# Splitting the weights behind the mixers once and keeping both parts in DRAM, in a hybrid decoder layer

## The chip, the cores and the metric

One core of a Trainium2 chip runs the whole program. The metric is device time in microseconds (us) from one launch. Before the change three runs took 3306.91, 3300.41 and 3303.79 us; the median is 3303.79. The profile comes from one more execution of 3299.76 us.

## The reference, cut to what matters

One layer of a decoder trunk over 2048 prompt tokens (and 8 sample tokens, one step each), width 1024:

```python
x = x + concat[mLSTM heads, S5 channel groups, gated-DeltaNet heads](rmsnorm(x) @ w_in) @ w_out
x = x + cross_attn(x)      # 4 heads into 256 memory tokens: softmax(q k) v, then w_mo
x = x + (silu(h @ w_gate) * (h @ w_up)) @ w_down      # h = rmsnorm(x), inner width 2816
y = rmsnorm(x)
```

Everything is float32. The mixers carry a state along the tokens; the S5 output also passes a gate with the weights w_glu. What comes behind the mixers (w_glu, w_out, cross attention, FFN) works on each token alone, with the same weights for all tokens.

## The kernel before, in words

The prompt is cut into four segments of 512 tokens, and the activations lie feature by token, so a weight tile of 128 partitions is the stationary operand of a matmul and up to 512 tokens stream past it. First come the memory keys and values and the w_in products of all four segments (`win`), with two folds in between that multiply memory keys and values into w_mq and w_mo (results Ad and Bd, in DRAM). Then `post` runs four times, once for each segment: w_glu, w_out, scores and values with Ad and Bd, then the FFN in six chunks of four or three tiles of gate and up, each chunk followed by its part of w_down. The mixers (`mlstm`, `gdn`, `s5`) and the attention of the sample tokens are generators; `tick` steps them between the matrix products, so that their small operations fall beside the large ones. In the trace post(0) runs from about 836 us, post(1) from 1483, post(2) from 2162 and post(3) from 2759 to the end. The mixers of segments 1, 2 and 3 and half of S5 run beside post(0), post(1) and post(2); beside post(3) there are none.

A float32 product is made of three float32r products: both operands are split into a high part (rounded to float32r) and a low part (the rest), and `gemm3` computes high x high, high x low and low x high into one PSUM tile. So each weight tile of up to 128 x 1024 is loaded raw into `wr` (L286 to L289), cast into `wh` on ScalarE (L292), and the low part `wl` is the difference wr - wh, on GpSimd or, for the first two tiles and those of index over 360, on VectorE (L293). `wr`, `wh` and `wl` have three buffers each. All weight tiles stand in one list `WL` of 512 entries in the order of use: 116 for `win`, memory and folds, then 103, 103, 95 and 95 for the four posts. `load_w` hands out tile i, makes the split of tile i + 2 and starts raw loads up to two tiles ahead of that. So a weight used in all four posts is loaded and split four times.

All transfers are issued by SyncE (SP), one queue whose instructions go in the order in which they stand; an instruction that waits holds those behind it. The order of each engine's instructions is set when the program is built, by a scheduler with a model of times; loads and splits of weights are put in with raised priority (`HP`). On the chip each engine then keeps its order and waits on semaphores.

Names: `H`, `X` are split activations, `x` the residual tiles, `t` temporaries, `acc` sums of squares, `P` and `M` PSUM tiles, `TB`, `big`, `g`, `m`, `mR` mixers' tiles, `gyd` and `mixd` the mixers' outputs in DRAM. L152 is `TT` (tensor_tensor on any engine), L155 `STT` (scalar_tensor_tensor on VectorE), L164 `mm`.

Of the kernel before, what the change touches and what calls it, by code (L numbers as in the profile page):

```python
# [6 lines left out]
F32 = mybir.dt.float32  # L7
# [6 lines left out]
MUL, ADD, SUB, MAX, MIN, POW = ALU.mult, ALU.add, ALU.subtract, ALU.max, ALU.min, ALU.pow  # L14
# [52 lines left out]
def build(ctx, tc, I, O):  # L67
    nc = tc.nc
    V, S, G, PE, SY = nc.vector, nc.scalar, nc.gpsimd, nc.tensor, nc.sync
# [14 lines left out]
    def nm(s):  # L84
        uid[0] += 1
        return f"{s}{uid[0]}"
# [4 lines left out]
    def dtile(shape, name):  # L91
        return dr.tile(shape, F32, name=name, tag=name)
# [58 lines left out]
    def TT(eng, out, a, b, op):  # L151
        eng.tensor_tensor(out=out, in0=a, in1=b, op=op)  # L152
# [64 lines left out]
    Ad = dtile([8, 128, 1024], "Ad")  # L217
    Bd = dtile([8, 128, 1024], "Bd")
# [49 lines left out]
    WL, wst, raws, splits = [], {"r": 0, "s": 0, "u": 0}, {}, {}  # L268

    def w_raw():  # L270
        with tc.high_priority(offset=HP):
            w_raw_()

    def w_split():
        with tc.high_priority(offset=HP):
            w_split_()

    def w_raw_():
        i = wst["r"]
        src, n = WL[i]  # L280
        raw = wp.tile([128, WN], F32, name=nm("wr"), tag="wr", bufs=3)
        src(raw)
        raws[i] = raw
        wst["r"] += 1

    def w_split_():  # L286
        i = wst["s"]
        n = WL[i][1]
        raw = raws.pop(i)  # L289
        wh = wp.tile([128, WN], F32R, name=nm("wh"), tag="wh", bufs=3)  # L290
        wl = wp.tile([128, WN], F32R, name=nm("wl"), tag="wl", bufs=3)
        S.copy(wh[:, 0:n], raw[:, 0:n])  # L292
        TT(V if i < 2 or i > 360 else G, wl[:, 0:n], raw[:, 0:n], wh[:, 0:n].bitcast(F32), SUB)  # L293
        splits[i] = (wh, wl)
        wst["s"] += 1

    def load_w():
        i = wst["u"]
        wst["u"] += 1
        while wst["s"] <= i + 2 and wst["s"] < len(WL):  # L300
            while wst["r"] <= wst["s"] + 2 and wst["r"] < len(WL):
                w_raw()
            w_split()
        return splits.pop(i)

    def plain(src, n=1024):
        WL.append((lambda raw: SY.dma_start(raw[:, 0:n], src), n))

    def gemm3(P, n, W, wofs, X, b0, bn, ks, mid=None, m=128, first=True, last=True):
        wh, wl = W  # L310
# [70 lines left out]
    def wl_win(extra=None):  # L381
        for n in range(18):
            plain(I["wF"][n])
            if extra is not None:
                extra(n)
        for g0, g1_ in ((0, 3), (3, 6), (6, 8)):
            plain(I["wTM"][:, g0:g1_, :].rearrange("p k c -> p (k c)"), (g1_ - g0) * 272)

    pre = {}
# [1069 lines left out]
    def wl_mem(i):  # L1459
        plain(I["wmk"][i] if i < 8 else I["wmv"][i - 8])  # L1460
# [3 lines left out]
    def mem_load():  # L1464
        mem["x"] = []
        for kk in range(4):
            x = xt()
            SY.dma_start(x[:, 0:512].rearrange("p (k c) -> p k c", k=2),
                         I["memT"][kk * 256:(kk + 1) * 256, :].rearrange("(k p) c -> p k c", p=128))
            mem["x"].append(x)  # L1470
            if kk in (0, 2):
                w_raw_()
# [89 lines left out]


    def wl_post(seg):
        for n in range(2):
            plain(I["wglu"][n])
        for n in range(8):
            plain(I["wout"][n])

        for h in range(4):  # L1570
            for i in range(2):
                plain(Ad[2 * h + i])
            for i in range(2):
                if seg == 0:
                    plain(I["wmq"][h, i])
                if seg == 1:
                    plain(I["wmo"][h, i])
        for n in range(3):
            plain(Bd[n, :, 0:768], 768)
        WL.append((lambda raw: SY.dma_start(raw[:, 0:768].rearrange("p (n c) -> p n c", n=3),  # L1580
                                            Bd[0:3, :, 768:1024].rearrange("n p c -> p n c")), 768))
        for n in range(3, 8):
            plain(Bd[n])
        for ci, (f0, fn) in enumerate(FCH):
            for f in range(f0, f0 + fn):
                if f != f0 or ci == 0:
                    plain(I["wgate"][f])
                plain(I["wup"][f])
            if ci + 1 < len(FCH):
                plain(I["wgate"][f0 + fn])  # L1590
            for n in range(0, 8, 2):
                def dn(raw, n=n, f0=f0, fn=fn):
                    SY.dma_start(raw[:, 0:2 * fn * 128].rearrange("p (a m) -> p a m", a=2),
                                 I["wdown"][n:n + 2, :, f0 * 128:(f0 + fn) * 128].rearrange("a p m -> p a m"))
                WL.append((dn, 2 * fn * 128))

    def hsplit(src, T, scale=None):
        h, l = ht(), ht()
# [368 lines left out]
    for i in range(NSEG):  # L1967
        wl_post(i)
# [265 lines left out]
```

## Time and profile before

| what | value |
|---|---|
| median of three runs | 3303.79 us |
| profiled execution | 3299.76 us, span 3298.0 us |
| PE busy | 3063.1 us, 93% of the span, 18202 matmuls |
| PEld, weight loads into PE | 2619.2 us, 79% |
| DVE busy | 2337.6 us, 71% |
| ACT busy | 1114.5 us, 34% |
| POOL busy | 1103.8 us, 33% |
| mean granted TensorE clock | 0.966 |
| DMA | 451.58 MB, mean 137 GB/s; the hardware queue 45.7% of 16 engines |

A busy share is the part of the span in which an engine had an instruction under way. Matmuls are pipelined, so two of them overlap and a busy PE is not always a PE at its peak. The clock is the granted share of the full TensorE clock, a mean over a stretch between the two levels of 2.4 GHz (1.00) and 1.2 GHz (0.50). The DMA share is the mean over the 16 DMA engines of the time that their packets took.

### The profile page before, as it was taken

The numbers are of one execution on the slowest core, as the hardware profiler recorded it, in microseconds if no ns is written. First come the engines' busy times: TensorE is split into PE (matmuls) and PEld (weight loads), VectorE is DVE, ScalarE is ACT, GpSimd is POOL, SyncE is SP. The second block draws the span as 40 slices with busy tenths as digits, with TensorE's granted clock in tenths as the row PEclk, the third lists the DMA queues.
The fourth block names the chain that finished last, engine by engine and source line by source line (L and its number), as shares of the span: only waits on it lengthen the run. The fifth ranks groups of instructions, "written<-read, shape, count | busy, mean of one in ns | idle before, by whom it ended". The sixth has DMA issues, their size and how long they took to land.

```text
span 3298.0 us, 49267 instructions
## 1 busy us (share of the span) xinstructions
PE 3063.1 (93%) x18202; PEld 2619.2 (79%) x18202; DVE 2337.6 (71%) x4746; ACT 1114.5 (34%) x1882; POOL 1103.8 (33%) x706
## 2 busy tenths in 40 slices
PE   7777889999888998998999999989999999999998
PEld 6676678778877776787789999978777877888886
DVE  8783695786788689668886787687766767554445
ACT  3123433422542332234432322244324224332222
POOL 6332545534354444444544444344411000000000
PEclk9887999999999999999999999999999999999999
DMA  6679666666445345335443444352333325222332
GB/s 208 176 183 206 205 184 212 200 193 173 144 129 182 90 122 166 103 111 168 144 121 117 125 124 125 100 164 84 105 94 108 104 90 182 88 91 95 96 90 77
DMA packets 361361, 451.58 MB, mean 137 GB/s; under 512 B 144820, under 2 KB 246556, under 8 KB 361120
## 3 DMA queue, kind: packets, MB, share of 16 engines
q1 hardware_dynamic: 361120, 448.43, 45.7%
q8 instruction: 144, 2.36, 0.3%
q14 instruction: 97, 0.79, 0.1%
HBM read 378.73 MB, written 71.73 MB: 137 GB/s over the span
## 4 chain that ended last, share of the span: by engine, by line
PE 61%; DVE 13%; issue 3%; ACT 2%; DMA 2%; SPq 0%; POOL 0%; DVEq 0%; POOLq 0%; ACTq 0%
PE P L164 54%; PE M L164 5%; DVE t L155 3%; DVE big L152 3%; DVE x L152 1%; DVE s5h L155 1%; DVE TB L155 1%; DVE acc L152 1%; ACT wh L292 1%; DMA t<-mixd 1%; DVE x L155 1%; DVE H L152 0%; DVE H L155 0%; DMA x<-in_xT 0%; DMA ABd<-AW 0%
## 5 line engine op out<-in xcount | busy, mean ns | idle before, releaser
L164 PE MATMUL P<-H,wh 128*128 128x512 f32 (+2 forms) x8032 | 2190.0, 360 | 80.1 <-DVE t L152 32.7
L164 PEld LDWEIGHTS P<-H,wh 128*128 128x128 f32 x8032 | 1419.4, 191 | 309.4 <-issue 30.9
L164 PE MATMUL P<-H,wl 128*128 128x512 f32 (+2 forms) x4016 | 1430.8, 357 | 13.8 <-POOL wl L152 13.8
L152 POOL TENSOR_TENSOR wl<-wr,wh 128x1024 fp32r<-128x1024 f32 (+2 forms) x359 | 863.5, 2409 | 970.4 <-ACT wh L292 861.7
L292 ACT CAST wh<-wr 128x1024 fp32r<-128x1024 f32 (+3 forms) x512 | 521.1, 1020 | 1198.1 <-PE P L164 705.1
L164 PEld LDWEIGHTS P<-H,wl 128*128 128x128 f32 x4016 | 766.9, 191 | 124.6 <-POOL wl L152 16.3
L152 DVE TENSOR_TENSOR x<-x,P 128x512 f32<-128x512 f32 (+2 forms) x312 | 181.2, 587 | 141.9 <-PE P L164 128.9
L152 DVE TENSOR_TENSOR big<-big,big 32x87 f32<-32x87 f32 (+16 forms) x500 | 249.6, 499 | 18.7 <-DMA big<-ABd 10.8
L164 PE MATMUL P<-wh,H 128*128 128x256 f32 (+1 forms) x1280 | 244.6, 289 | 8.2 <-ACT pp L1717 6.3
L152 DVE TENSOR_TENSOR t<-P,R 128x512 f32<-128x512 f32 (+2 forms) x190 | 109.6, 581 | 165.7 <-PE P L164 142.0
L152 POOL TENSOR_TENSOR rs<-rcol,mhalf 128x4 f32<-128x4 f32 (+2 forms) x17 | 20.7, 1218 | 598.5 <-DVE rcol L161 598.2
L164 PEld LDWEIGHTS P<-wh,H 128*128 128x128 f32 x1280 | 204.7, 193 | 12.0 <-ACT pp L1717 8.2
L152 DVE TENSOR_TENSOR wl<-wr,wh 128x1024 fp32r<-128x1024 f32 (+1 forms) x153 | 183.8, 1202 | 25.5 <-ACT wh L292 22.8
L164 PE MATMUL P<-wl,H 128*128 128x256 f32 (+1 forms) x640 | 183.0, 287 | 0.5 <-POOL wl L152 0.5
L155 DVE SCALAR_TENSOR_TENSOR t<-P,R 128x512 f32<-128x512 f32 (+1 forms) x120 | 69.6, 583 | 153.9 <-PE P L164 152.2
L155 DVE SCALAR_TENSOR_TENSOR t<-t,t 128x512 f32<-128x512 f32 (+3 forms) x140 | 146.7, 1052 | 37.5 <-ACT t L1830 23.2
L152 DVE TENSOR_TENSOR H<-t,H 128x512 fp32r<-128x512 f32 (+1 forms) x120 | 123.5, 1037 | 46.3 <-ACT H L1600 46.2
L164 PEld LDWEIGHTS P<-wl,H 128*128 128x128 f32 x640 | 123.6, 193 | 1.2 <-POOL wl L152 0.7
L1600 ACT CAST H<-t 128x512 fp32r<-128x512 f32 (+1 forms) x120 | 73.5, 621 | 141.7 <-DVE t L152 124.8
L155 DVE SCALAR_TENSOR_TENSOR t<-g,VEC,t 128x256 f32<-128x256 f32 x144 | 99.5, 691 | 20.0 <-ACT t L724 18.4
L155 DVE SCALAR_TENSOR_TENSOR H<-x,VEC,H 128x512 fp32r<-128x512 f32 (+2 forms) x104 | 102.2, 996 | 8.5 <-ACT H L334 6.6
L152 DVE TENSOR_TENSOR acc<-acc,t 128x512 f32<-128x512 f32 (+1 forms) x115 | 99.1, 861 | 9.2 <-ACT t L343 7.3
(414 smaller groups left out, 3114.7 us busy)
## 6 DMA issues: line engine op xcount, KB each, us to landing
wr<-in_wgate SPq DMA_DIRECT2D x88, 512.0 KB
wr<-in_wup SPq DMA_DIRECT2D x88, 512.0 KB
wr<-in_wF SPq DMA_DIRECT2D x72, 512.0 KB
wr<-in_wdown SPq DMA_DIRECT2D x64, 512.0 KB
TB<-TB SPq DMA_DIRECT2D x64, 417.0 KB
wr<-in_wout SPq DMA_DIRECT2D x32, 512.0 KB
wr<-Ad SPq DMA_DIRECT2D x32, 512.0 KB
zf<-t SPq DMA_DIRECT2D x56, 256.0 KB
```

Source lines behind the costliest of these rows:

```text
L152: eng.tensor_tensor(out=out, in0=a, in1=b, op=op)
L155: V.scalar_tensor_tensor(out=out, in0=a, scalar=s, in1=b, op0=op0, op1=op1, **kw)
L164: PE.matmul(out, l, r, start=st, stop=sp)
L292: S.copy(wh[:, 0:n], raw[:, 0:n])
L1600: S.copy(h[:, 0:T], src[:, 0:T])
```

## The change

The weights of the posts that every segment uses (w_glu, w_out, Ad, Bd, w_gate, w_up, w_down: 95 tiles of a post) are split in post(0) only. There both parts are also stored into DRAM tiles `ws_...` (mode "store"). In post(1), post(2) and post(3) no raw tile is loaded for them; both parts are loaded from DRAM, straight into `wh` and `wl` (mode "pre"). The tiles of `win`, memory and folds, and the eight tiles of wmq in post(0) and of wmo in post(1), keep their raw load and their split (mode "raw"). Subtractions that are left go to GpSimd but for the first two tiles.

```diff
--- before.py
+++ after.py
@@ -277,22 +277,38 @@
 
     def w_raw_():
         i = wst["r"]
-        src, n = WL[i]
+        wst["r"] += 1
+        src, n, key, mode = WL[i]
+        if mode == "pre":
+            return
         raw = wp.tile([128, WN], F32, name=nm("wr"), tag="wr", bufs=3)
         src(raw)
         raws[i] = raw
-        wst["r"] += 1
 
     def w_split_():
         i = wst["s"]
-        n = WL[i][1]
-        raw = raws.pop(i)
+        src, n, key, mode = WL[i]
         wh = wp.tile([128, WN], F32R, name=nm("wh"), tag="wh", bufs=3)
         wl = wp.tile([128, WN], F32R, name=nm("wl"), tag="wl", bufs=3)
-        S.copy(wh[:, 0:n], raw[:, 0:n])
-        TT(V if i < 2 or i > 360 else G, wl[:, 0:n], raw[:, 0:n], wh[:, 0:n].bitcast(F32), SUB)
+        if mode == "pre":
+            for q, t in enumerate((wh, wl)):
+                SY.dma_start(t[:, 0:n].bitcast(F32), wsd(key, n)[q])
+        else:
+            raw = raws.pop(i)
+            S.copy(wh[:, 0:n], raw[:, 0:n])
+            TT(V if i < 2 else G, wl[:, 0:n], raw[:, 0:n], wh[:, 0:n].bitcast(F32), SUB)
+            if mode == "store":
+                for q, t in enumerate((wh, wl)):
+                    SY.dma_start(wsd(key, n)[q], t[:, 0:n].bitcast(F32))
         splits[i] = (wh, wl)
         wst["s"] += 1
+
+    WSD = {}
+
+    def wsd(key, n):
+        if key not in WSD:
+            WSD[key] = dtile([2, 128, n], "ws_" + "_".join(str(q) for q in key))
+        return WSD[key]
 
     def load_w():
         i = wst["u"]
@@ -303,8 +319,8 @@
             w_split()
         return splits.pop(i)
 
-    def plain(src, n=1024):
-        WL.append((lambda raw: SY.dma_start(raw[:, 0:n], src), n))
+    def plain(src, n=1024, key=None, mode="raw"):
+        WL.append((lambda raw: SY.dma_start(raw[:, 0:n], src), n, key, mode))
 
     def gemm3(P, n, W, wofs, X, b0, bn, ks, mid=None, m=128, first=True, last=True):
         wh, wl = W
@@ -1562,37 +1578,37 @@
 
 
     def wl_post(seg):
+        mode = "store" if seg == 0 else "pre"
         for n in range(2):
-            plain(I["wglu"][n])
+            plain(I["wglu"][n], key=("u", n), mode=mode)
         for n in range(8):
-            plain(I["wout"][n])
-
+            plain(I["wout"][n], key=("o", n), mode=mode)
         for h in range(4):
             for i in range(2):
-                plain(Ad[2 * h + i])
+                plain(Ad[2 * h + i], key=("A", 2 * h + i), mode=mode)
             for i in range(2):
                 if seg == 0:
                     plain(I["wmq"][h, i])
                 if seg == 1:
                     plain(I["wmo"][h, i])
         for n in range(3):
-            plain(Bd[n, :, 0:768], 768)
+            plain(Bd[n, :, 0:768], 768, ("B", n), mode)
         WL.append((lambda raw: SY.dma_start(raw[:, 0:768].rearrange("p (n c) -> p n c", n=3),
-                                            Bd[0:3, :, 768:1024].rearrange("n p c -> p n c")), 768))
+                                            Bd[0:3, :, 768:1024].rearrange("n p c -> p n c")), 768, ("B", 8), mode))
         for n in range(3, 8):
-            plain(Bd[n])
+            plain(Bd[n], key=("B", n), mode=mode)
         for ci, (f0, fn) in enumerate(FCH):
             for f in range(f0, f0 + fn):
                 if f != f0 or ci == 0:
-                    plain(I["wgate"][f])
-                plain(I["wup"][f])
+                    plain(I["wgate"][f], key=("g", f), mode=mode)
+                plain(I["wup"][f], key=("p", f), mode=mode)
             if ci + 1 < len(FCH):
-                plain(I["wgate"][f0 + fn])
+                plain(I["wgate"][f0 + fn], key=("g", f0 + fn), mode=mode)
             for n in range(0, 8, 2):
                 def dn(raw, n=n, f0=f0, fn=fn):
                     SY.dma_start(raw[:, 0:2 * fn * 128].rearrange("p (a m) -> p a m", a=2),
                                  I["wdown"][n:n + 2, :, f0 * 128:(f0 + fn) * 128].rearrange("a p m -> p a m"))
-                WL.append((dn, 2 * fn * 128))
+                WL.append((dn, 2 * fn * 128, ("d", ci, n), mode))
 
     def hsplit(src, T, scale=None):
         h, l = ht(), ht()
```

The instructions as they stand on three queues. On POOL, near the start of the FFN of post(1), about 1700 us (`wl` is the low part of a weight tile, `ms` belongs to the S5 scan, `m` and `mR` to mLSTM). Before:

```order
L152 TENSOR_TENSOR wl_16155<-wr_16054,wh_16154 128x1024
L152 TENSOR_TENSOR ms_16129<-gs_16124,TB_15904 128x128
L152 TENSOR_TENSOR wl_16199<-wr_16087,wh_16198 128x1024
L152 TENSOR_TENSOR m_16260<-m_15159,eex_15431 128x260
L159 TENSOR_SCALAR m_16384<-m_16384 128x256
L152 TENSOR_TENSOR m_16399<-m_16395,mhalf 128x4
L152 TENSOR_TENSOR wl_16266<-wr_16152,wh_16265 128x1024
L152 TENSOR_TENSOR wl_16337<-wr_16196,wh_16336 128x1024
L152 TENSOR_TENSOR ms_16319<-gs_16314,TB_16114 128x128
```

Now, around the same mLSTM step:

```order
L152 TENSOR_TENSOR ms_16366<-gs_16361,TB_16149 128x128
L152 TENSOR_TENSOR m_16493<-m_15418,eex_15686 128x260
L152 TENSOR_TENSOR m_16628<-m_16624,mhalf 128x4
L159 TENSOR_SCALAR m_16613<-m_16613 128x256
L152 TENSOR_TENSOR ms_16550<-gs_16545,TB_16351 128x128
L152 TENSOR_TENSOR ms_16724<-gs_16719,TB_16535 128x128
```

The weights' subtractions are gone from between the mixers' operations, and these follow each other. On SP, near the end of the FFN of post(0) (`wr` raw weights, `ws` the new DRAM tiles, `mixd` and `zv` the mixers' data). Before:

```order
L307 DMA wr_14056<-in_wup 128x1024
L1593 DMA wr_14093<-in_wdown 128x2x384
L1593 DMA wr_14129<-in_wdown 128x2x384
L583 DMA m_15159<-zv 128x4x64
L1593 DMA wr_14175<-in_wdown 128x2x384
```

Now:

```order
L302 DMA ws_p_14405<-wh_14401 128x1024
L599 DMA m_15418<-zv 128x4x64
L302 DMA ws_p_14405<-wl_14402 128x1024
L1609 DMA wr_14448<-in_wdown 128x2x384
L590 DMA mixd<-m_14426 128x2x128
L302 DMA ws_d_0_14454<-wh_14450 128x768
L302 DMA ws_d_0_14454<-wl_14451 128x768
L1609 DMA wr_14487<-in_wdown 128x2x384
```

Each raw load now has two stores of an earlier tile ahead of it, which wait for the cast and for the subtraction. On SP, at the start of post(2), about 2150 us (`t<-gyd` are inputs of the gate behind S5, `out_yT` the stores of the segment before). Before:

```order
L307 DMA wr_22318<-in_wout 128x1024
L307 DMA wr_22374<-in_wout 128x1024
L307 DMA wr_22430<-in_wout 128x1024
L1609 DMA t_22437<-gyd 128x512
L1609 DMA t_22474<-gyd 128x512
L307 DMA wr_22539<-in_wout 128x1024
L1609 DMA t_22546<-gyd 128x512
L307 DMA wr_22617<-in_wout 128x1024
```

Now:

```order
L295 DMA wh_22517<-ws_o_8609 128x1024
L295 DMA wl_22518<-ws_o_8609 128x1024
L1625 DMA t_22522<-gyd 128x512
L1625 DMA t_22559<-gyd 128x512
L295 DMA wh_22624<-ws_o_8705 128x1024
L295 DMA wl_22625<-ws_o_8705 128x1024
L1625 DMA t_22629<-gyd 128x512
L1625 DMA t_22652<-gyd 128x512
L295 DMA wh_22700<-ws_o_8821 128x1024
L295 DMA wl_22701<-ws_o_8821 128x1024
L1897 DMA out_yT<-x_14860 128x512
```

A tile is two transfers in place of one, and fewer tiles have been asked for when the same `t<-gyd` stands: one tile of w_out ahead of the first instead of three.

## Rows read from the trace of the kernel before

**Rows 1.** Page, busy us (share of span) and instructions by engine.
```profile
PE 3063.1 (93%) x18202; PEld 2619.2 (79%) x18202; DVE 2337.6 (71%) x4746; ACT 1114.5 (34%) x1882; POOL 1103.8 (33%) x706
```

**Rows 2.** Windows: stretch, busy PE, PEld, DVE, ACT, POOL, clock, DMA share, GB/s.
```profile
0.00:836.00 836.00, 711.94 (x4305) 612.45 (x4306) 592.68 (x1521) 272.35 (x493) 371.29 (x263) 0.92 0.69 195
1038.00:1483.00 445.00, 423.98 (x2105) 335.24 (x2104) 331.56 (x587) 135.68 (x216) 191.35 (x105) 0.97 0.41 125
1238.00:1338.00 100.00, 87.51 (x452) 68.36 (x450) 93.52 (x167) 27.17 (x43) 43.44 (x22) 0.93 0.52 155
1483.00:1600.00 117.00, 104.01 (x580) 86.76 (x579) 101.95 (x171) 57.71 (x110) 60.81 (x38) 0.97 0.49 161
1600.00:2162.00 562.00, 546.79 (x4447) 521.03 (x4446) 432.76 (x936) 180.00 (x303) 248.12 (x156) 0.98 0.41 122
2162.00:2323.00 161.00, 143.26 (x863) 123.19 (x861) 124.89 (x233) 65.65 (x131) 66.44 (x40) 0.97 0.38 119
2323.00:2759.00 436.00, 434.80 (x2192) 347.06 (x2192) 292.21 (x544) 148.06 (x232) 63.55 (x51) 1.00 0.35 104
2759.00:2900.00 141.00, 137.38 (x803) 120.03 (x802) 89.64 (x145) 58.72 (x101) 2.38 (x2) 1.00 0.38 128
2900.00:3270.00 370.00, 370.00 (x1600) 299.54 (x1599) 186.02 (x231) 99.28 (x119) 1.92 (x1) 1.00 0.30 91
```

**Rows 3.** Page, groups of instructions: busy us, mean ns, idle before.
```profile
L152 POOL TENSOR_TENSOR wl<-wr,wh 128x1024 fp32r<-128x1024 f32 (+2 forms) x359 | 863.5, 2409 | 970.4 <-ACT wh L292 861.7
L292 ACT CAST wh<-wr 128x1024 fp32r<-128x1024 f32 (+3 forms) x512 | 521.1, 1020 | 1198.1 <-PE P L164 705.1
L152 DVE TENSOR_TENSOR wl<-wr,wh 128x1024 fp32r<-128x1024 f32 (+1 forms) x153 | 183.8, 1202 | 25.5 <-ACT wh L292 22.8
```

**Rows 4.** Groups by shape on DVE, 1483 to 2162 us.
```profile
L152 DVE TENSOR_TENSOR H<-t,H 128x520 fp32r<-128x520 f32 x22 | 35.6, 1617 | 12.4 <-ACT H L1600 12.3
L155 DVE SCALAR_TENSOR_TENSOR t<-t,t 128x520 f32<-128x520 f32 x22 | 31.3, 1421 | 9.2 <-ACT t L1830 9.1
```

**Rows 5.** The same view, 2405 to 2759 us.
```profile
L152 DVE TENSOR_TENSOR H<-t,H 128x512 fp32r<-128x512 f32 x26 | 17.5, 683 | 4.9 <-ACT H L1600 4.9
L155 DVE SCALAR_TENSOR_TENSOR t<-t,t 128x512 f32<-128x512 f32 x18 | 12.6, 702 | 2.0 <-ACT t L1830 2.0
```

**Rows 6.** Waits of PE, 1483 to 2162: total us, times, longest.
```profile
PE P L164 <- DVE x L152: 8.9, 4, 4.7
```

**Rows 7.** Waits of PE, 2162 to 2759.
```profile
PE M L748 <- DVE t L155: 5.7, 1, 5.7
PE M L743 <- ACT t L735: 5.5, 3, 2.9
```

**Rows 8.** Windows: the busiest 5 us of the DMA engines.
```profile
2793.00:2798.00 5.00, 5.00 (x24) 4.04 (x22) 4.50 (x7) 3.01 (x5) 0.00 (x0) 1.00 1.01 392
```

**Rows 9.** Chain that ended last, two pieces: start us, us, what.
```profile
939.48 3.60 DMA wr<-in_wmq
...
2929.16 348.90 PE P L164 x1503
```

**Rows 10.** Waits over the whole span, one of ACT.
```profile
ACT wh L292 <- DMA wr<-in_wF: 78.6, 16, 11.0
```

**Rows 11.** Waits of the SP queue, 1483 to 2162.
```profile
SPq L307 <- POOL wl L152: 215.1, 59, 8.3
SPq L1212 <- PE M L164: 56.6, 22, 6.4
```

**Rows 12.** Timeline of SP: one weight transfer issued, start us, us.
```profile
2200.42 0.33 SPq L307 DMA_DIRECT2D wr<-Ad  x1
```

## The prediction

> **What bounds the kernel now.** I read the page's busy shares first, then the table of windows by stage, then who waited for whom on PE, and last the DVE groups by shape. PE is busy for 93% of the span [rows 1], but not evenly. In the table of windows [rows 2] the last long stretch, 2900 to 3270, has PE at 370.00 of 370.00 us and clock 1.00; the chain there is one piece of PE work, 1503 matmuls in 348.90 us [rows 9], 0.232 us each, so a weight tile of 24 matmuls is 5.57 us. Where it looks like that, no removed cast or subtraction can help. What can be won stands where PE idles or runs at the lower clock after a stall. From the first matmul of post(1), at 1483, to the end these are (idle = window less PE busy; clock = window times what PEclk lacks to 1.00): 1483 to 1600, 13.0 and 3.5; 1600 to 2162, 15.2 and 11.2; 2162 to 2323, 17.7 and 4.8; 2323 to 2759, 1.2 and 0; 2759 to 2900, 3.6 and 0 [rows 2].
>
> What makes PE wait there is DVE and what hangs on it: DVE x (x+P, which frees PSUM) for 8.9 us in post(1), the mixers' t from DVE and ACT for 5.7 and 5.5 us in post(2) [rows 6, 7]. And DVE is slow there. The product t<-t,t on 128x520 takes 1421 ns and H<-t,H 1617 ns while POOL subtracts weights [rows 4]; from 2405 on, where the subtraction is on DVE and POOL nearly idle, the same operations on 128x512 take 702 and 683 ns [rows 5]. Both read two SBUF tiles, as POOL's wl<-wr,wh does, 2409 ns each [rows 3].
>
> **The change part by part.** A list of 512 weight tiles is walked in order: 116 ahead of post(0), then 103, 103, 95 and 95 for the four post segments. 95 of each post segment (all but the 8 of wmq or wmo) are concerned, so 285 tiles lose their split.
>
> Removed: 285 ACT casts of 1020 ns, 291 us; of the subtractions 151 on DVE (index over 360) at 1202 ns, 181 us, and 134 on POOL at 2409 ns, 323 us [rows 3]. The DVE part lies after 2405, beside a PE that is full [rows 2], and is worth nothing by itself. The POOL part lies in 1483 to 2405, and its worth is what it gives back to DVE: in post(1) alone 22 x (1421 - 702) + 22 x (1617 - 683) = 36 us on two of DVE's forms [rows 4, 5]. ACT also no longer holds a cast at its queue's head until PE frees a slot.
>
> How much of that reaches PE? The measure is a stretch without contention. 2759 to 2900 is the same kind of transition (end of one post, start of the next) with POOL idle, and costs 3.6 us of idle and no clock; 2323 to 2759 is an FFN with mixers and mostly without POOL weights, and costs 1.2 [rows 2]. So:
> - 1483 to 1600: 16.5 less 3.6 is 12.9 us at most; I take three quarters, 10.
> - 2162 to 2323: 22.5 less 3.6 is 18.9; three quarters, 13.
> - 1600 to 2162: 26.4 less 1.2 is 25 at most; the S5 scan also runs here, which needs DVE without any contention, so half, 13.
> - After 2323: 1. The tail behind the last matmul stays.
> Together 37 us, with bounds of 0 and 58.
>
> Added in post(0): 190 stores of up to 512 KB. From 1038 to 1483 (69 tiles, 6.4 us each) they are 70 MB, 158 GB/s on top of 125, so 283; at 1238 to 1338, where the decode attention streams its cache, 155 + 164 = 319 GB/s [rows 2]. In the busiest 5 us the DMA engines moved 392 GB/s at share 1.01 [rows 8], so there would be room. In the quiet stretch 91 GB/s cost a share of 0.30 [rows 2], which makes 303 GB/s a full share, and then 319 does not fit. No stretch of this trace is full of large stores, so this is bounded: below by 0 (the raw loads run some three tiles ahead, and a store has two tile times until its slot is wanted), above by the first rival, 59 us. What I take: queues get longer and the mixers' trips through DRAM with them. PE's loss in 1038 to 1483 is now 21.0 idle + 13.4 clock; a third more is 12 us (nearest row: 0.69 of share in 0 to 836, with the clock at 0.92 [rows 2]).
> The Trainium skill (HBM Reference, Specifications) gives about 425 GB/s for a core that streams alone and 358 for its share of a pair. By that rule 283 and 319 both fit, this term is nearly 0, and the sum would be -32 instead of -20; the 392 agrees with it for loads, and no run here shows it for stores.
>
> Added in post(1) to post(3): 285 more loads, 48 MB a segment, 71 to 89 GB/s more, so about 200 GB/s, what 0 to 836 carries now (195 GB/s, share 0.69 [rows 2]). A part is loaded straight into the slot that PE has just left: the load for tile k can go when PE ends k-3 and must land before k starts, two tiles or 11.1 us later (8.4 for tiles of 18 matmuls). One load lands in 3.60 us [rows 9]; two, with 2 x 0.33 us of issue [rows 12] and 1.3 us for the second 512 KB at 392 GB/s, about 5.6. So 5 us of margin, where the raw load had a tile more and the split behind it. Behind a waiting load on SP stand the mixers' transfers and the y stores and x loads of a transition; but SP stood just so before, 215.1 us in post(1) for POOL's wl [rows 11], which came one split after the same PE event. Ahead of a load can stand a transfer that waits itself: 56.6 us in 22 waits for PE in the S5 steps alone [rows 11], 2.6 us on average, under the margin. In 0 to 836, at equal DMA load, ACT waited 16 times, 4.9 us each, for w_in tiles [rows 10]. Lower bound 0, upper bound 8 such waits reaching PE, 39 us; I take one, 5 us.
> SP's 475 more issues of 0.33 us are 157 us of an engine that mostly waits: nothing.
>
> Sum: -37 + 12 + 5 = -20 us on the profiled execution, 3299.8 us (span 3298.0). That execution lies 4.0 us under the median of the runs, 3303.8, so the median becomes 3283.8; I say 3284.
>
> **Rivals.**
> *DMA is full in post(0).* If large stores beside the loads hold the engines to c GB/s, the 445 us from 1038 stretch by 445 x (283/c - 1). At c = 250 that is 59 us, which with the gain kept and late loads as above gives 3303.8 - 37 + 59 + 5 = 3331: slower. It decides against the change from c below some 265. For it: 303 GB/s to a full share in the quiet stretch. Against: 392 for 5 us, and 320 GB/s or more is asked only in the attention's 100 us.
> *The loads become the new wait.* SP is one queue in fixed order, and with one tile less ahead PE stands for wh or wl. At 39 us it eats the gain: 3303.8 - 37 + 12 + 39 = 3318; with four of 4.9 us, 3298. For it: 16 late w_in loads at equal DMA load. Against: in the posts no load was late by more than a few us, and PE waited for POOL's wl, which came after it, hardly at all.
> *DVE's relief stays off the path.* The stalls belong to chains through DRAM, PSUM and DVE's order, which the change leaves; then only a quarter of the 58 is won, 15, less 12 + 5: 3306, no change.
> *All of it is won.* 58 us and no loss: 3246.
>
> **How the numbers follow.** Forecast (3284, own range 3262 to 3296) 0.56; all won 0.07; DMA full 0.13; late loads 0.12; relief off the path 0.12. The schedule is made anew with every edit, and PE's and DVE's orders shift with it; that widens each case by some 10 us and is in the ranges. Range for 8 in 10: from between the forecast and the best case, 3250, to just under the DMA case, 3326. Changes under 0.2% (6.6 us) can't be told from none here. Faster: 0.56 and 0.07, less 0.04 of the forecast's tail, plus 0.03 of late loads: 0.62. Same: 0.04 + 0.09 of the last rival + 0.03 of late loads: 0.16. Slower: 0.22.
>
> **What would show it.** Right: t<-t,t and H<-t,H at about 700 ns in post(1); PE idle and clock in the two transitions near 4 us each; no PE wait on a DMA of wh or wl over a few us; post(0) longer by 10 to 15 us, with the DMA share near 0.8. Wrong: PE waits named DMA wh<-ws in number (second rival); post(0) longer by 40 us or more, shares at 1 from 1038 on (first); DVE's forms fast but PE's idle unchanged (third).

## The result, and the profile after

The changed kernel takes 3255.39 us (median of 4 runs, 3248.39 to 3256.57) where before took 3303.1 beside it (4 runs): a ratio of 0.9853, 95% interval 0.984 to 0.9866, or 47.7 us less. The forecast was 3284, 20 us less; the direction and the range (3250 to 3326) held, but the gain that I forecast is under half of the measured one.

The length of each stage, from the first matmul of its first weight tile to that of the next stage's (post(3): to the last matmul with a weight), read off the matmuls of each trace (us; experiments, told below, are entered here too). By this measure post(0) begins at 840.0 us before and post(1) at 1487.3, some 4 us behind the 836 and 1483 given ahead of the prediction. Post(0)'s FFN is counted from the same matmul in every trace, the first of the last Bd tile, one tile (24 matmuls) ahead of w_gate's. From trace to trace with the same work, post(2) and post(3) agree within about 2 us, post(1) within about 4 (651.8 after, 655.8 in e4), the win stages within 13 (840.0 before, 852.6 in e1).

| kernel | ratio to before | win | post(0): to FFN + FFN | post(1) | post(2) | post(3) |
|---|---|---|---|---|---|---|
| before | 1 | 840.0 | 197.3 + 450.0 | 674.5 | 596.8 | 523.6 |
| after | 0.9853 | 843.2 | 201.9 + 440.4 | 651.8 | 576.5 | 524.9 |
| e1 POOL kept busy | 0.9998 | 852.6 | 201.9 + 441.9 | 676.0 | 598.8 | 524.6 |
| e2 before, DVE splits from post(1) | 0.9890 | 849.3 | 194.2 + 450.0 | 649.2 | 585.4 | 523.6 |
| e3 stores alone | 0.9972 | 850.6 | 202.3 + 438.3 | 672.4 | 594.7 | 523.6 |
| e8 tiny stores alone | 1.0013 | 851.2 | 194.6 + 459.2 | 676.7 | 594.0 | 523.6 |
| e6 stores twice | 1.0234 | 849.8 | 219.5 + 541.6 | 653.1 | 576.0 | 525.2 |
| e4 after, w_in too | 0.9810 | 828.1 | 196.5 + 440.8 | 655.8 | 577.2 | 524.5 |
| e5 after, DVE splits from post(0) | 0.9750 | 847.8 | 181.7 + 420.9 | 653.2 | 577.0 | 523.9 |
| e9 = e4 with e5 | 0.9721 | 836.6 | 183.3 + 420.8 | 653.0 | 577.0 | 524.4 |
| e10 before, DVE splits from post(0) | 0.9768 | 850.1 | 182.1 + 429.2 | 649.5 | 585.4 | 523.6 |
| e11 before, all splits on DVE | 0.9642 | 802.7 | 183.5 + 426.2 | 647.7 | 586.4 | 523.7 |
| e12 after, all splits on DVE | 0.9598 | 807.5 | 178.2 + 420.4 | 649.4 | 577.3 | 524.0 |
| e13 = e12, w_in too | 0.9604 | 805.9 | 181.8 + 421.5 | 651.5 | 576.7 | 525.2 |

So after has +3.2 ahead of post(0), -5.0 in it, -22.7 in post(1), -20.3 in post(2), +1.3 in post(3): -43.5 between two traces whose spans differ by 43.3.

The page's busy line after, and its two groups of weight splits, answer to [rows 1, 3]:

```profile
PE 3059.5 (94%) x18202; PEld 2619.2 (80%) x18202; DVE 1993.0 (61%) x4595; ACT 840.7 (26%) x1597; POOL 775.6 (24%) x572
...
L152 POOL TENSOR_TENSOR wl<-wr,wh 128x1024 fp32r<-128x1024 f32 (+3 forms) x225 | 541.3, 2411 | 636.6 <-ACT wh L298 575.6
L298 ACT CAST wh<-wr 128x1024 fp32r<-128x1024 f32 (+3 forms) x227 | 231.1, 1021 | 448.4 <-PE P L164 221.6
```

The 285 casts and 285 subtractions are gone. The windows by stage answer to [rows 2]:

```profile
843.00:1045.00 202.00, 175.40 (x1228) 161.55 (x1228) 161.59 (x326) 87.91 (x166) 93.27 (x51) 0.92 0.72 247
1045.00:1485.00 440.00, 426.14 (x2125) 337.01 (x2125) 344.16 (x624) 137.07 (x221) 193.18 (x105) 0.99 0.84 295
1485.00:1600.00 115.00, 108.30 (x637) 91.62 (x636) 77.83 (x178) 43.71 (x91) 23.92 (x24) 0.97 0.69 238
1600.00:2137.00 537.00, 533.18 (x4370) 509.74 (x4369) 320.80 (x921) 100.01 (x218) 50.36 (x72) 0.99 0.59 198
2137.00:2278.00 141.00, 139.00 (x864) 120.67 (x863) 91.48 (x241) 47.93 (x113) 14.32 (x18) 1.00 0.63 212
2278.00:2714.00 436.00, 434.83 (x2193) 346.98 (x2192) 212.93 (x484) 75.24 (x156) 25.76 (x36) 1.00 0.55 190
```

Read three things. The transition into post(2) is clean: 2.0 us of PE idle in 141, clock 1.00, where it was 17.7 us and 0.97 [rows 2]. Post(0)'s FFN moves 295 GB/s instead of 125 at a share of 0.84 and is not longer. In post(2)'s FFN DVE has 79 us less to do than in the like window of before and PE, full in both, gains nothing: 434.83 of 436 us against 434.80.

The whole of post(1), first before, then after, in the same view:

```profile
1487.00:2162.00 675.00, 646.80 (x5008) 604.52 (x5007) 530.71 (x1103) 233.99 (x405) 305.40 (x191) 0.98 0.42 128
```
```profile
1485.00:2137.00 652.00, 641.48 (x5005) 601.36 (x5004) 398.62 (x1099) 143.72 (x309) 74.29 (x95) 0.99 0.61 205
```

DVE executes the same 1100 instructions in 398.62 us instead of 530.71: it lost no work there, its instructions got faster on average. Two of its forms in 1485 to 2137 [rows 4 for before]:

```profile
L152 DVE TENSOR_TENSOR H<-t,H 128x520 fp32r<-128x520 f32 x22 | 15.3, 698 | 9.5 <-ACT H L1616 9.4
L155 DVE SCALAR_TENSOR_TENSOR t<-t,t 128x520 f32<-128x520 f32 x22 | 15.3, 697 | 7.1 <-ACT t L1846 7.0
```

What PE waits for from 1485 to 2278 (us in all, times, longest) [rows 6, 7 for before]:

```profile
PE P L164 <- DMA wh<-ws_A: 4.1, 3, 2.1
PE P L164 <- ACT pp L1733: 2.3, 3, 0.8
PE P L164 <- DMA wh<-ws_o: 2.1, 1, 2.1
PE M L164 <- DVE mR L152: 2.1, 1, 2.1
PE P L164 <- DMA wl<-ws_o: 0.7, 1, 0.7
```

DVE x, 8.9 us before, is no longer among them. Late parts are, for some 7 us (two more such rows have 0.5 and 0.3). The SP queue shows how they come about at the start of a post:

```profile
1497.40 0.38 SPq L295 DMA_DIRECT2D wl<-ws_o  x1
...
1505.13 1.44 SPq L1897 DMA_DIRECT2D out_yT<-x  x3
...
1508.64 4.55 SPq L1674 DMA_DIRECT2D x<-in_xT  x6
1513.99 0.33 SPq L295 DMA_DIRECT2D wh<-ws_o  x1
```

Between 1497.4 and 1514.0 no part is issued: the y stores and x loads of the transition stand ahead. That is the margin the prediction spoke of, spent once.

### The profile page after: what moved, and what is told of

Its sections match the earlier page's. It is cut to its first block, busy times and chain, and to the rows that moved or that the text cites. A ratio compares the mean times of both kernels' runs of the same rounds, so it can differ in the third digit from the quotient of the medians.

```text
span 3254.7 us, 49325 instructions
## 1 busy us (share of the span) xinstructions
PE 3059.5 (94%) x18202; PEld 2619.2 (80%) x18202; DVE 1993.0 (61%) x4595; ACT 840.7 (26%) x1597; POOL 775.6 (24%) x572
## 4 chain that ended last, share of the span: by engine, by line
PE 67%; DVE 7%; DMA 3%; issue 2%; ACT 1%; POOL 1%; SPq 0%; POOLq 0%; DVEq 0%; ACTq 0%
PE P L164 60%; PE M L164 6%; DVE t L155 1%; DVE big L152 1%; DMA t<-mixd 1%; POOL wl L152 1%; DVE x L152 0%; DVE s5h L155 0%; DVE acc L152 0%; DVE H L155 0%; DMA wl<-ws_o 0%; DMA wh<-ws_B 0%; ACT wh L298 0%; DVE TB L155 0%; ACT H L1616 0%
## 5 line engine op out<-in xcount | busy, mean ns | idle before, releaser
L152 POOL TENSOR_TENSOR wl<-wr,wh 128x1024 fp32r<-128x1024 f32 (+3 forms) x225 | 541.3, 2411 | 636.6 <-ACT wh L298 575.6
L298 ACT CAST wh<-wr 128x1024 fp32r<-128x1024 f32 (+3 forms) x227 | 231.1, 1021 | 448.4 <-PE P L164 221.6
L152 DVE TENSOR_TENSOR big<-big,big 32x87 f32<-32x87 f32 (+16 forms) x500 | 219.4, 439 | 26.6 <-DMA big<-ABd 18.1
L155 DVE SCALAR_TENSOR_TENSOR t<-t,t 128x512 f32<-128x512 f32 (+3 forms) x140 | 109.8, 788 | 63.6 <-ACT t L1846 41.9
L152 DVE TENSOR_TENSOR H<-t,H 128x512 fp32r<-128x512 f32 (+1 forms) x120 | 89.6, 753 | 67.4 <-ACT H L1616 67.2
L1846 ACT ACTIVATE t<-t 128x512 f32<-128x512 f32 (+1 forms) x88 | 55.7, 633 | 279.3 <-DVE t L152 279.0
L152 POOL TENSOR_TENSOR ms<-gs,TB 128x128 f32<-128x128 f32 x64 | 32.8, 512 | 374.9 <-PE M L164 123.1
L155 DVE SCALAR_TENSOR_TENSOR H<-x,VEC,H 128x512 fp32r<-128x512 f32 (+2 forms) x104 | 94.4, 921 | 10.2 <-ACT H L350 7.6
```

The source lines that it names most:

```text
L155: V.scalar_tensor_tensor(out=out, in0=a, scalar=s, in1=b, op0=op0, op1=op1, **kw)
L1846: S.activation(th[:, 0:Tb], gt[:, 0:Tb], AF.Tanh, scale=0.5)
```

## The experiments

The theory: POOL's subtractions slow DVE wherever they run beside it, DVE holds PE up at the stalls, and transfers have room. The rivals: the gain came from ACT's casts, the order or the way slots are filled; or DMA sets a price. The experiments ran beside a before of 3309.5 to 3310.4 us, so ratios are compared, not times.

**e1: parts as in the change, POOL kept busy.**
```diff
             for q, t in enumerate((wh, wl)):
                 SY.dma_start(t[:, 0:n].bitcast(F32), wsd(key, n)[q])
+            if i <= 360:
+                sc = wp.tile([128, WN], F32, name=nm("wr"), tag="wr", bufs=3)
+                TT(G, sc[:, 0:n], wh[:, 0:n].bitcast(F32), wl[:, 0:n].bitcast(F32), SUB)
```


> The changed kernel, and for each weight tile up to index 360 that comes as parts GpSimd does a subtraction of the two parts into a scratch tile that nobody reads: POOL works as before, while the loads of parts, the missing ACT casts and everything else stay. Theory (POOL's subtractions slow DVE, and PE waits on DVE in post(1) and post(2)): t<-t,t on 128x520 goes from 697 back to some 1400 ns, post(1) from 652 back towards 672 us and post(2) from 577 towards 594, in all 3285 to 3300. Rival (what was won came from ACT's queue, from the order of the instructions or from the slots that are filled by DMA): DVE is slow again, but post(1) and post(2) stay within 5 us of 652 and 577, in all 3250 to 3265.

Measured: 3309.4, ratio 0.9998 (0.9988 to 1.0007). The gain is gone, all of it, in post(1) (676.0) and post(2) (598.8). Windows of these two stages:

```profile
1497.00:2173.00 676.00, 648.90 (x5006) 605.05 (x5005) 508.07 (x1096) 141.39 (x306) 301.82 (x192) 0.98 0.59 199
2173.00:2771.00 598.00, 580.63 (x3049) 471.30 (x3048) 347.19 (x724) 123.19 (x268) 131.55 (x92) 0.99 0.56 189
```

POOL's added subtractions in them, by shape:

```profile
L152 POOL TENSOR_TENSOR wr<-wh,wl 128x1024 f32<-128x1024 f32 x118 | 290.2, 2460 | 325.9 <-DMA wl<-ws_p 78.3 <-DMA wl<-ws_g 71.0 <-DMA wl<-ws_d 48.2
```

ACT is as light as after the change (141.39 us), POOL as heavy as before, and DVE needs 508.07 us for 1096 instructions. POOL's added reads also hold the slots of the parts longer, so late parts are a rival here. Three of PE's waits from 1497 to 2771 speak against it:

```profile
PE P L164 <- DVE x L152: 11.4, 8, 3.0
PE M L767 <- DVE t L155: 9.6, 3, 6.0
...
PE P L164 <- DMA wh<-ws_A: 2.3, 2, 1.2
```

All waits for parts make 4.6 us there, fewer than after the change, and the longest are again for DVE. So the casts, the fewer POOL results that PE waits for and the filling by DMA are not the cause. Two expectations missed: the loss is all of the gain and not most of it, and t<-t,t did not go back to 1400 ns (869 here); the subtractions fell on other DVE work.

**e2: before, only the subtractions of post(1) and later on DVE.**
```diff
-        TT(V if i < 2 or i > 360 else G, wl[:, 0:n], raw[:, 0:n], wh[:, 0:n].bitcast(F32), SUB)
+        TT(V if i < 2 or i > 218 else G, wl[:, 0:n], raw[:, 0:n], wh[:, 0:n].bitcast(F32), SUB)
```


> The kernel before, with one number changed: all subtractions behind post(0) (index over 218 instead of over 360) go to DVE, so POOL has none of them and no transfer is added. Theory (contention): t<-t,t on 128x520 falls from 1421 to about 700 ns, and post(1) and post(2) win most of what the change won there, less what 134 subtractions of 1.2 us cost DVE itself: in all 3265 to 3285 against 3303. Rival (ACT's casts and the order): the casts are still there, so nothing is won, and DVE has 161 us more: 3300 to 3330.

Measured: 3273.39, ratio 0.989 (0.9873 to 0.9906), 36 us less than before with no transfer changed. Post(1) in the windows view:

```profile
1493.00:2143.00 650.00, 639.55 (x5009) 600.27 (x5008) 494.60 (x1205) 235.64 (x406) 62.11 (x87) 0.99 0.45 133
```

Two of DVE's groups by shape in it:

```profile
L152 DVE TENSOR_TENSOR wl<-wr,wh 128x1024 fp32r<-128x1024 f32 x92 | 113.5, 1235 | 16.7 <-ACT wh L292 15.8
...
L155 DVE SCALAR_TENSOR_TENSOR t<-t,t 128x520 f32<-128x520 f32 x22 | 15.2, 689 | 0.1
```

DVE takes 92 whole and 12 narrower subtractions on and is still busy for less time, 494.60 us against 530.71. Post(1) takes 649.2, where it takes 651.8 with parts: relief alone gives all that the change won there. The 2.6 us between them are within the scatter of this stage, so a price of late parts beyond PE's waits of 7.7 us is not shown. In post(2) moving the work gives 11.4 of the 20.3 us. The other 9 lie ahead of its FFN (171.9 us in e2, 163.2 after) and come with DVE not having the subtractions, ACT not having the casts or another order, which these two kernels don't separate.

**e3 and e8: stores alone, whole and tiny.** Before, with post(0)'s parts stored and not read; in e8 only 16 columns of each. The diff is cut to the stores, and its comments name the run.
```diff
+            if mode == "store":
+                for q, t in enumerate((wh, wl)):
+                    SY.dma_start(wsd(key, n)[q], t[:, 0:n].bitcast(F32))             # e3
+                    SY.dma_start(wsd(key, n)[q][:, 0:16], t[:, 0:16].bitcast(F32))   # e8, in its place
```


> The kernel before, and in post(0) each concerned weight tile's two parts are stored to DRAM as in the changed kernel; nobody reads them, the later segments load raw tiles and split them as before. The prediction's term: the stores lengthen post(0) by some 12 us: 3312 to 3318. Rival one (the stores are free, and what post(0) won in the changed kernel has another cause): post(0) 647 and in all 3300 to 3306. Rival two (the stores, or the order that they bring, are what made post(0)'s FFN shorter): post(0) about 640, in all 3293 to 3299.

> The kernel before, with stores of both parts in post(0) as in the run with stores alone, but of 16 of the columns only: as many instructions and almost the same order of them, 1/64 of the bytes. It asks why post(0)'s FFN got 10 us shorter with stores. Theory (the order of the instructions and the later moment at which a slot comes free, so that POOL's subtractions fall elsewhere against DVE's work): post(0) about 641 as with full stores, in all 8 to 10 us under before. Rival (the transfers themselves, by keeping POOL or the caches of the decode attention slower): 647 us as before, no difference in all.

Measured: e3 3300.73, 0.9972 (0.9961 to 0.9984), post(0) 640.6; e8 3312.75, 1.0013 (1.0004 to 1.0022), post(0) 653.8. Post(0)'s FFN in e3, then in e8:

```profile
1053.00:1491.00 438.00, 425.57 (x2125) 337.18 (x2124) 344.16 (x622) 138.22 (x222) 196.22 (x107) 0.99 0.84 295
```
```profile
1046.00:1505.00 459.00, 433.67 (x2126) 341.90 (x2125) 340.10 (x605) 139.04 (x222) 194.62 (x107) 0.96 0.45 128
```

96 MB of stores made the program a little faster, not slower, as rival two of e3 had it; the same number of small ones did not. Two of DVE's groups in post(0)'s FFN, before and after:

```profile
L155 DVE SCALAR_TENSOR_TENSOR s5h<-TB,s5h 128x256 f32<-128x256 f32 x63 | 44.1, 700 | 1.5 <-DMA TB<-in_cvl 0.2
L155 DVE SCALAR_TENSOR_TENSOR t<-t,t 128x512 f32<-128x512 f32 x22 | 37.2, 1689 | 9.6 <-ACT t L1830 9.5
```
```profile
L155 DVE SCALAR_TENSOR_TENSOR s5h<-TB,s5h 128x256 f32<-128x256 f32 x63 | 50.0, 794 | 2.5 <-DMA TB<-in_cvl 1.5
L155 DVE SCALAR_TENSOR_TENSOR t<-t,t 128x512 f32<-128x512 f32 x22 | 28.4, 1291 | 8.2 <-ACT t L1846 8.2
```

With whole stores POOL's subtractions fall more on the decode attention, that of the sample tokens (s5h, for which PE waits 0.4 us), and less on the FFN's t. But e8 does not have the order of e3, so it does not test the order alone: the scheduler, which has a model of times, places the decode attention later on DVE when the stores are whole. Of its 64 first products these fall into post(0)'s FFN before, in e3 and in e8:

```profile
L155 DVE SCALAR_TENSOR_TENSOR TB<-TB,s5h 128x256 f32<-128x256 f32 x25 | 15.8, 677 | 0.0
```
```profile
L155 DVE SCALAR_TENSOR_TENSOR TB<-TB,s5h 128x256 f32<-128x256 f32 x42 | 28.1, 714 | 0.0
```
```profile
L155 DVE SCALAR_TENSOR_TENSOR TB<-TB,s5h 128x256 f32<-128x256 f32 x32 | 18.3, 620 | 0.1
```

PE's longest wait in the FFN before and in e8, and the same wait in e3:

```profile
PE P L164 <- ACT H L1600: 9.0, 1, 9.0
```
```profile
PE P L164 <- ACT H L1616: 9.9, 1, 9.9
```
```profile
PE P L164 <- ACT H L1616: 4.4, 1, 4.4
```

Its waits there for DVE's H go the same way: 5.2, 6.4 and 0.5 us. Whether the other order or the bytes shorten the FFN was not separated. It does not hang on POOL's subtractions: with these on DVE the FFN takes 420.9 us with stores (e5) and 429.2 without (e10), 420.4 (e12) and 426.2 (e11), and the decode attention moves there too (52 of its products in the FFN of e5, 20 in that of e10).

**e5: the change, and what is left from post(0) on split on DVE.**
```diff
-            TT(V if i < 2 else G, wl[:, 0:n], raw[:, 0:n], wh[:, 0:n].bitcast(F32), SUB)
+            TT(V if i < 2 or i > 115 else G, wl[:, 0:n], raw[:, 0:n], wh[:, 0:n].bitcast(F32), SUB)
```


> The changed kernel, and the subtractions that are left in post(0) and post(1) (103 and 8 tiles, index over 115) go from POOL to DVE. Theory (contention is what costs, in post(0) too): t<-t,t on 128x512 falls there from 1291 to about 700 ns, post(0) gets 5 to 15 us shorter than its 642 us, in all 3240 to 3252 on a chip where before takes 3303. Rival (DVE is the bound there: it is busy for 344 of 440 us in post(0)'s FFN, beside the decode attention, and gets 70 subtractions of 1.2 us, 84 us more): post(0) 5 to 30 us longer, 3260 to 3285.

Measured: 3224.27, ratio 0.975 (0.9735 to 0.9764). Post(0) falls from 642.3 to 602.7, far more than I expected. Its two windows:

```profile
848.00:1024.00 176.00, 162.22 (x1200) 150.45 (x1200) 134.28 (x317) 86.30 (x163) 13.66 (x17) 0.98 0.78 270
1024.00:1450.00 426.00, 424.58 (x2150) 339.21 (x2148) 325.37 (x729) 137.31 (x216) 32.26 (x37) 1.00 0.87 306
```

Three of DVE's groups by shape in the second:

```profile
L152 DVE TENSOR_TENSOR wl<-wr,wh 128x1024 fp32r<-128x1024 f32 x61 | 74.4, 1220 | 5.9 <-ACT wh L298 5.6 <-DMA wr<-in_wup 0.2
L155 DVE SCALAR_TENSOR_TENSOR s5h<-TB,s5h 128x256 f32<-128x256 f32 x63 | 31.4, 499 | 3.6 <-DMA TB<-in_cvl 2.9
...
L155 DVE SCALAR_TENSOR_TENSOR t<-t,t 128x512 f32<-128x512 f32 x22 | 16.1, 732 | 1.0 <-ACT t L1846 0.9
```

The second window starts one tile (24 matmuls) ahead of the FFN as the table has it. PE is full there (424.58 of 426 us, clock 1.00) with stores beside the loads at 306 GB/s.

**e6: each part stored twice in post(0).**
```diff
                     SY.dma_start(wsd(key, n)[q], t[:, 0:n].bitcast(F32))
+                    SY.dma_start(wsd(key + ("x",), n)[q], t[:, 0:n].bitcast(F32))
```


> The changed kernel, and each part is stored twice in post(0), the second time into DRAM that nobody reads. That asks 295 + 158, some 450 GB/s, of post(0)'s FFN, where the changed kernel moved 295 at a share of 0.84 and in its fullest 50 us 367 at 1.01. Theory (the DMA engines do have a limit near 370 to 390 GB/s, the change just stays under it): the 440 us of the FFN stretch to 440 x 450/380, some 520, in all 3315 to 3345. Rival (stores cost PE nothing even then, the slots and queues cover it): post(0) within 10 us of 642, in all 3250 to 3265.

Measured: 3383.41, ratio 1.0234 (1.0218 to 1.025); the FFN takes 541.6 us. Its window:

```profile
1069.00:1611.00 542.00, 464.51 (x2152) 356.59 (x2151) 316.45 (x669) 138.23 (x222) 187.92 (x106) 0.93 0.99 377
```

The two longest waits of PE in it:

```profile
PE P L164 <- POOL wl L152: 31.6, 27, 1.9
PE P L164 <- ACT wh L298: 21.1, 12, 5.6
```

Here is the limit that the first rival put at 250 or so: 377 GB/s at share 0.99. The loss is larger than I expected (some 520 us for the FFN, 3345 at most in all). Over its FFN the change stays a fifth under that limit; only in the first 50 us does it move 374 GB/s at share 1.02, with PE busy for 48.86 of them. PE waits for splits in e6; of these the casts wait 63.6 us for raw loads (16.3 after the change) and 15.3 us for stores. The Trainium skill (HBM Reference, Specifications) gives 425 GB/s for a core that streams alone and 358 for its share of a pair; 377 GB/s, loads and stores mixed, lies between.

**e4, e9: parts for w_in too, then with e5's edit as well.** The diff is cut to the part for w_in.
```diff
-    def wl_win(extra=None):
-            plain(I["wF"][n])
+    def wl_win(extra=None, mode="pre"):      # "store" in the first segment; w_TM's three tiles alike
+            plain(I["wF"][n], key=("F", n), mode=mode)
```


> The changed kernel, and the same is done for the 21 weight tiles of w_in: parts stored in the first segment's win stage, loaded as parts in the three others. That takes 63 casts and 63 subtractions of 2.4 us out of the first 843 us and adds 43 MB there, 51 GB/s on top of 195 to 247, so a DMA share of about 0.85. Theory (contention on DVE is what costs, transfers have room): the win stages end 10 to 30 us sooner, in all 3225 to 3245. Rival (there the loads themselves are late: ACT waited 16 times 4.9 us for w_in tiles, and now twice the bytes must come, with one tile less ahead): the stages are 5 to 30 us longer, in all 3260 to 3285.

> The changed kernel with parts for w_in too (which alone gave a ratio of 0.981), and with post(0)'s and post(1)'s remaining subtractions on DVE. Theory (contention): both gains add up, a ratio of 0.976 to 0.979. Rival (DVE is the bound in post(0)): 0.983 to 0.990.

Measured: e4 3247.6, 0.981 (0.9789 to 0.983); e9 3214.15, 0.9721 (0.9705 to 0.9737). The window of e4's win stages:

```profile
0.00:828.00 828.00, 712.41 (x4340) 615.19 (x4340) 525.60 (x1526) 216.71 (x436) 222.07 (x201) 0.93 0.88 261
```

And one of PE's waits in it:

```profile
PE P L164 <- DMA wh<-ws_F: 15.6, 4, 5.5
```

Both happen: DVE needs 525.60 us for nearly the same number of instructions, where it took 592.68 [rows 2], and parts are late for 15.6 us at a share of 0.88.

**e10 to e13: no parts at all, and no POOL at all.** e10 and e11 are before with the index at 115, and with DVE for every tile; e12 and e13 the change and e4 with DVE for every tile (there the line goes out that the change had put in).
```diff
-        TT(V if i < 2 or i > 360 else G, wl[:, 0:n], raw[:, 0:n], wh[:, 0:n].bitcast(F32), SUB)
+        TT(V if i < 2 or i > 115 else G, wl[:, 0:n], raw[:, 0:n], wh[:, 0:n].bitcast(F32), SUB)   # e10
+        TT(V, wl[:, 0:n], raw[:, 0:n], wh[:, 0:n].bitcast(F32), SUB)                              # e11 to e13
```


> The kernel before, with one number changed: every subtraction from post(0) on (index over 115 instead of over 360) on DVE, no parts in DRAM. With the subtractions of post(1) on moved, the ratio was 0.989, and moving post(0)'s in the changed kernel gave 39 us there. Theory (POOL beside DVE is the whole cost, parts in DRAM add little): both add up, a ratio of 0.976 to 0.980, against 0.975 for the same with parts. Rival (DVE, with casts and subtractions still to do, becomes late without the parts): 0.983 to 0.990.

> The kernel before with all 512 subtractions on DVE, none on POOL. Theory: the win stages too are held up by contention (PE idle 124 of 840 us, clock 0.92) and win 10 to 30 us on top of the kernel with those from post(0) on moved: 0.967 to 0.974. Rival (DVE is the bound there: busy 595 of 840 us, and gets 114 subtractions of 1.2 us, 137 us, more): 10 to 40 us longer than that kernel, 0.980 to 0.992.

> The changed kernel with all the subtractions that are left on DVE. The same question for the win stages as in the kernel before with all on DVE, with parts in post(1) to post(3): by contention 0.965 to 0.972, by the rival (DVE the bound of the win stages) 0.978 to 0.990; 0.975 is what moving those from post(0) on gave.

> The kernel with parts for w_in too (0.972 with post(0)'s subtractions on DVE) and all the rest on DVE: there are 53 tiles left in the win stages instead of 116, 64 us more for a DVE that is busy 526 of 828 us. Theory (contention): 0.963 to 0.970. Rival (DVE is the bound, the first segment has 37 of them in a row): 0.973 to 0.985.

Measured: e10 3235.16, 0.9768 (0.9753 to 0.9783); e11 3192.45, 0.9642 (0.9625 to 0.9659); e12 3178.69, 0.9598 (0.9581 to 0.9615); e13 3181.6, 0.9604 (0.9584 to 0.9623). The theory's ranges hold e10; e5, e9, e11, e12 and e13 gained more than it said. So moving every subtraction, with no DRAM parts, is worth 118 us, over twice the change. Parts on top of it (e12 against e11) add 0.4%, parts of w_in nothing that shows. e12 is the fastest kernel here, with e13 level with it.

The order of the instructions is made anew in every kernel, so no pair alone rules it out. But the stages fall into two groups through all of them: post(1) takes 672.4 to 676.7 us where GpSimd subtracts beside it throughout (before, e1, e3, e8) and 647.7 to 655.8 in the ten others; post(0) takes 637.3 us or more where it does and 598.6 to 611.3 in the six others; the win stages take 840.0 to 852.6 with all their subtractions but two on GpSimd and 802.7 to 807.5 with none.

e11's page has this busy line:

```profile
PE 3032.4 (95%) x18202; PEld 2607.8 (82%) x18202; DVE 2220.4 (70%) x5105; ACT 1119.1 (35%) x1882; POOL 255.4 (8%) x347
```

Three of its groups on DVE over the whole span:

```profile
L152 DVE TENSOR_TENSOR wl<-wr,wh 128x1024 fp32r<-128x1024 f32 (+3 forms) x512 | 612.6, 1198 | 88.2 <-ACT wh L292 82.7 <-PE M L1727 3.2 <-issue 0.2
L152 DVE TENSOR_TENSOR x<-x,P 128x512 f32<-128x512 f32 (+2 forms) x312 | 181.6, 588 | 140.3 <-PE P L164 130.8 <-DMA x<-in_xT 6.0 <-issue 1.7
...
L152 DVE TENSOR_TENSOR H<-t,H 128x512 fp32r<-128x512 f32 (+1 forms) x120 | 81.8, 688 | 21.5 <-ACT H L1600 21.3
```

The last two of these in the kernel before:

```profile
L152 DVE TENSOR_TENSOR x<-x,P 128x512 f32<-128x512 f32 (+2 forms) x312 | 181.2, 587 | 141.9 <-PE P L164 128.9 <-DMA x<-in_xT 10.6 <-DVE x L152 0.7
...
L152 DVE TENSOR_TENSOR H<-t,H 128x512 fp32r<-128x512 f32 (+1 forms) x120 | 123.5, 1037 | 46.3 <-ACT H L1600 46.2
```

DVE does 359 subtractions more and is busy for 2220.4 us instead of 2337.6 [rows 1]. x<-x,P, which reads one operand from PSUM, takes 587 and 588 ns; H<-t,H, both from SBUF, 1037 and 688. The Trainium skill (SBUF — State Buffer, Who interferes with whom) has just that: a DVE operation with two SBUF inputs contends with GpSimd reading SBUF, and one with at most one, outside DVE's 2-port perf modes, does not. The trace agrees.

## Why the prediction was right, and where it was wrong

*What bounds the kernel* was right: POOL beside DVE, seen as the same form at 1421 and 702 ns. e1 puts the cause back and the gain is gone; e2 takes it away without the change and most of the gain is there.

*The step that failed is the loss in post(0), +12 us for the stores.* Post(0) got 5.0 us shorter in the change and 6.7 with the stores alone, so the term was 17 us off, most of the distance between forecast and result. I took DMA share as proportional to GB/s (91 at 0.30, so 303 for a full share) and then a third more stall for longer queues. The rows show 295 GB/s at 0.84 and 377 at 0.99, so share is not proportional to GB/s; and at 0.84 the stores added no stall that shows, so the lower bound, 0, was the better choice. The "nearest row" that I leaned on, 0.69 with the clock at 0.92 in the win stages [rows 2], owes part of its stalls to POOL's subtractions: without them e11 and e12 run those stages in 803 to 808 us at a share of 0.75. PE still idles there for 100 of e11's 803 us, at a clock of 0.93; what causes that stays open. That post(0) got shorter instead of staying as it was no part of the prediction foresaw.

*Late loads, +5 us:* about 7.7 us of PE waits in post(1) and its neighbour; the 2.6 us by which e2's post(1) is shorter are within the scatter. Right mechanism, and a size that fits; the second rival fails.

*The gains.* Post(1): predicted 10 + 13, less the 5; measured 22.7 net, so somewhat more. Into post(2): predicted 13 of at most 18.9; the stage up to its FFN went from 183.5 to 163.2, all 20.3 us, since 2.0 us of idle and no clock loss are left where my cap still had 3.6 of idle. The three quarters were a mean between all and half for which no row spoke, and three quarters of 18.9 are 14, not 13. By e2 the moved subtractions give 11.4 of the 20.3, so 13 was about right for what it stood for; the other 9 came only where the parts were there as well, for which the prediction had no term. After 2323: predicted 1; measured 0.0 in post(2)'s FFN (413.3 both) and 1.3 longer in post(3). The 151 subtractions taken off DVE there were worth nothing, as said.

*Sum by stages:* the gains were -45.6 (e2's -25.3 in post(1), -20.3 in post(2)) for -37, the stores -5.0 for +12, the late parts, if e2's 2.6 are theirs, +2.6 for +5; with +4.5 ahead of post(0) and in post(3) that is the -43.5 of the traces.

*The rivals.* DMA full: refuted, e6 reaches 377 GB/s and not 250 to 303. Relief off the path: refuted by e1 and e2. "All won", 3246, was nearest to the mark: its assumption of no loss was right, its 58 us of gain were not reached (45.6), and the shorter post(0) made up part of that by luck.

What I did not see: post(0) and the win stages were held up by the same thing. They stood in the same page, POOL busy for 191.35 of 445 us and 371.29 of 836 [rows 2], and I counted only the stages where the change took it away. They were worth some 40 us each (e5, e11).

Open: whether the other order or the bytes of the whole stores shorten post(0) (e3 against e8; by 11.1 us in e12 against e11, where POOL has no subtraction anyway), and why post(2) is 9 us shorter with parts even then (e12 against e11, all of it ahead of its FFN).

## What to carry to other kernels

Before moving work to GpSimd to spare DVE, compare DVE's busy time for the same instructions, those with two SBUF operands above all, in stretches with and without GpSimd running: here each of 359 subtractions spared DVE 1.2 us and cost 1.5 us of its other work on average (117 us less busy with 429 us of subtractions more). When a change removes the cause of a stall, look for every stage where that cause stands, and try the smallest edit that removes it alone. Price transfers by whether the DMA share stays near 1 over a stage, not by how much it rises: here a share of 0.84 added no stall that shows, and 0.99 made the FFN 101 us longer.

## What the runs showed of the hardware

Loads and stores mixed ran at 295 to 307 GB/s for over 400 us with PE busy for 97% of them or more (426.14 of 440 us at 295 after the change, 423.60 of 425 us at 307 in e12), and at 377 GB/s, share 0.99, when more was asked. The same subtraction of 128 x 1024 takes 2.4 us on GpSimd and 1.2 on DVE. The DVE form t<-t,t on 512 or 520 columns, some 680 to 730 ns without GpSimd's subtractions, took anywhere from 869 to 1689 with them in different kernels; the mean of one form is no measure of the contention, the busy time of all of DVE's instructions in the stage is (530.71 against 398.62 us for the same 1100).
